# Feed-forward up and gate by Strassen's seven products, and the down projection as its own stage

## The chip, the core and the metric

The kernel runs on one core of a Trainium2 chip. The core has a matrix engine (PE, with its weight loads shown as PEld), a vector engine (DVE), a scalar engine for activations and copies (ACT), a general engine (POOL) and an engine that issues most transfers (SP). They work side by side, each in the order of its own instruction list, and wait for each other by semaphores. Data lies in SBUF (128 partitions), PE writes its sums to PSUM, and weights and results lie in DRAM.

The metric is the device time of one execution in microseconds (us), lower is better. Before the change it is 1745.42 us, the median of 3 runs (1744.86 to 1748.16).

## What is computed

One inference step of a one-layer encoder over 1024 prompt tokens and 8 streams of 16 tokens: T = 1152 tokens of width 1024. Attention, a short convolution and a cross-attention come first; the change touches what follows the last residual sum, the gated feed-forward with its causal convolution over time:

```python
D_MODEL = 1024; D_FF = 2816; FFN_CONV_WIDTH = 3

def rms_norm(x, g):
    y = x * lax.rsqrt(jnp.mean(x * x, axis=-1, keepdims=True) + EPS)
    return y * g

def causal_dwconv(u, state, w):             # three taps over time
    full = jnp.concatenate([state, u], axis=1)
    y = w[0] * full[:, 0:t_len]
    for j in range(1, 3):
        y = y + w[j] * full[:, j:j + t_len]
    return y, full[:, -2:]

    x = x + xo.reshape(b, t_len, D_MODEL) @ w_xo
    hf = rms_norm(x, g_ffn)
    u_c, new_ffn = causal_dwconv(hf @ w_up, ffn_state, w_ffconv)
    x = x + (jax.nn.silu(u_c) * (hf @ w_gate)) @ w_down
    ...
    y = rms_norm(x, g_final)
```

Everything is float32. The streams bring their own two earlier rows (`ffn_state`), the prompt starts from zeros, and the last two up-projected rows of each go out as `new_ffn`.

## The kernel before

Activations lie transposed, with 128 features on the partitions and the 1152 tokens along the free axis. A float32 product is made of three PE passes: each operand is split into a high part (rounded by ACT to PE's format, `h`) and a low part (`l = x - h`, on DVE or POOL), and `mm3` (L142 to L144) sums `h*h`, `h*l` and `l*h` in one PSUM bank. A weight unit is 128x1024 numbers (512 KB): one transfer `raw` into one of two buffers, then two halves, each a cast `wh` on ACT (L107) and a subtraction `wl` (L108), on POOL and DVE in turn. `block` multiplies one unit (eight 128x128 weight tiles for one block of 128 output features) with all tokens in three chunks of 384 columns (`CH`), 24 matmuls a chunk.

`residual` (L734) adds the output of the last projection (`w_xo`) to the residual `x`, writes the sum to DRAM (`x2`), and keeps it times the gain as split pairs `hfh`, `hfl`. The factor `r3` (one over the root mean square of a token) comes only after all of it is done, so it is multiplied in at the end of the up and gate products.

The feed-forward has 22 blocks of 128 hidden features. `ffn_block(f)` (L954) runs an up block, a convolution and a gate block:

- up: each bank is taken by DVE with `r3` into a padded row `u` (`evac_padded`, L249); the convolution is one ACT operation for the first tap (L261) and two DVE operations of 1168 columns (L263) for the others; ACT applies silu (L965), and POOL multiplies `r3` in (L967 for the prompt, L968 for the streams).
- gate: DVE multiplies each bank by this row (L978) and the product is split into the pair `gp`.

The blocks are gathered in groups (`GROUPS`, 4, 4, 4, 4, 3 and 3 blocks). Behind the first block of the next group stands the down projection of a finished one: `ffn_down` (L984) multiplies its pairs with the weights `w_dn` and adds to `acc` (8x1152 numbers a partition, kept in SBUF, L1000). `ffn_last` (L1011) makes the last group's share chunk by chunk (512, 384 and 256 columns) with the residual sums, their squares, and the final normalisation (`norm`, L1029), which is interleaved with the next chunk's products.

The program order is that of the Python code; the framework places each instruction in its engine's list by its own estimate of when it can run, adds the semaphore waits, and gives buffers out in turn from pools (for `raw` 2 buffers, for `wh` and `wl` 3 each). A transfer into a buffer waits until its last reader is done.

Of the kernel before, what the change touches and what calls it, by code (L numbers as in the profile page):

```python
# [33 lines left out]
GROUPS = [4, 4, 4, 4, 3, 3]  # L34
# [16 lines left out]
class Step:  # L51
    def __init__(self, ctx, tc, I, O):
# [5 lines left out]
        self.open("const")  # L58
        self.open("small")
# [5 lines left out]
    def open(self, name, side="left", space=None):  # L65
        kw = {} if space else {"side": side, "reuse_waits": "tile"}
# [28 lines left out]
    def bank(self, tag):  # L95
        return self.tile("psum", tag, [1024 if tag == "sc" else 512], 2)

    def const(self, shape, src, dt=F32):
        t = self.tile("const", f"c{self.n}", shape, 1, dt)
# [10 lines left out]
    def wraw(self, src, spare=None):  # L110
        raw = spare or self.tile("weights", "raw", [1024], 2)
# [3 lines left out]
    def wunit(self, src, spare=None):  # L115

        raw = self.wraw(src, spare)
        hs, ls = [], []
        for i in range(2):
            h, l = self.tile("weights", "wh", [512], 3, F32R), self.tile("weights", "wl", [512], 3, F32R)  # L120
            self.lflip ^= 1
            self.split(h, l, raw[:, i * 512:(i + 1) * 512], self.nc.gpsimd if self.lflip else self.nc.vector)
# [149 lines left out]
    def setup(self):  # L272
        nc, I = self.nc, self.I
        nc.scalar.preload_act_table_set("natural_log_exp_and_others")
        self.g = self.const([5, KT], I["gains"])
        self.ones = self.const([P], None)
        nc.vector.memset(self.ones, 1.0)
        self.eps = self.const([1], None)
# [6 lines left out]
    def setup2(self):  # L285
# [9 lines left out]
        self.wff = self.const([NFB, 3], I["wff"])  # L295
# [3 lines left out]
    def lam(self):  # L299

        nc = self.nc
        l = self.tile("const", "lam", [4], p=QD)
        nc.sync.dma_start(out=l, in_=self.I["lam"])
        pr = self.tile("const", "lampr", [2], p=QD)
# [13 lines left out]
    def start(self):  # L318
# [4 lines left out]
        self.r1 = self.tile("x", "r", [T])  # L323
# [410 lines left out]
    def residual(self, wsrc, xh, xl, xsrc, dst, gi, pool):  # L734
# [4 lines left out]
        r = self.tile(pool, "r", [T])  # L739
# [214 lines left out]
    def ffn_block(self, f):  # L954
        nc, I = self.nc, self.I
        u = self.A(TPAD)
        st, new = self.tile("t8", "sff", [NB, 2], 2), self.tile("t8", "nff", [18], 2)
        nc.sync.dma_start(out=st, in_=I["sff"][f])
        self.pads(u, st)
        self.block(I["w_ug"][2 * f], self.hfh, self.hfl, "mm", self.evac_padded(u, self.r3))  # L960
        self.last_rows(new, u)
        self.nc.sync.dma_start(out=self.O["nff"][f], in_=new)
        s = self.A(TPAD)
        self.conv(s, u, self.wff[:, f])
        nc.scalar.activation(s[:, HALO:TPAD], s[:, HALO:TPAD], AF.Silu)  # L965
        seg = self.pseg(s)[:, :, HALO:]
        nc.gpsimd.tensor_tensor(out=self.pp(s), in0=self.pp(s), in1=self.r3[:, 0:S_P], op=ALU.mult)  # L967
        nc.gpsimd.tensor_tensor(out=seg, in0=seg, in1=self.r3[:, S_P:T].rearrange("p (b t) -> p b t", t=TS), op=ALU.mult)  # L968
        gt = self.A()
        h, l = self.tile("t8", "gp", [T], 10, F32R), self.tile("t8", "gp", [T], 10, F32R)  # L970

        def evac(c, ps):
            cs = slice(c * CH, (c + 1) * CH)
            for bs, view, by_stream in self.chunk_views(s, c):
                a, o = ps[:, bs], gt[:, c * CH + bs.start:c * CH + bs.stop]
                if by_stream:
                    a, o = (z.rearrange("p (b t) -> p b t", t=TS) for z in (a, o))
                nc.vector.tensor_tensor(out=o, in0=a, in1=view, op=ALU.mult)  # L978
            self.split(h[:, cs], l[:, cs], gt[:, cs])

        self.block(I["w_ug"][2 * f + 1], self.hfh, self.hfl, lambda c: ("tr", "tr", "mm")[c], evac)
        return h, l

    def ffn_down(self, g, parts):  # L984
# [288 lines left out]
```

## Time and profile before

| | us |
|---|---|
| median of 3 runs | 1745.42 |
| the profiled execution's own time | 1758.31 |
| its span in the trace | 1756.3 |
| PE busy in the span | 1718.8 (98%) |
| DVE / ACT / POOL busy | 836.7 / 561.1 / 370.6 |
| mean granted clock of PE | 0.991 |

The profile comes from one execution, which took 12.9 us more than the median of the runs. In it the feed-forward starts at 892.8 us, when the last matmul of the residual stage is done. A busy engine is one that executes; waiting is not counted. A row of a group gives the line, the engine, the operation, the tiles out<-in with their shape, the count, the busy time and the mean duration of one; behind the second bar stands how long the engine was idle just before, and what ended that. PE overlaps its matmuls, so the duration of one (0.34 us at 384 columns) is not what the next has to wait; the time from one start to the next is.

### The profile page before, as it was taken

The numbers are of one execution on the slowest core, as the hardware profiler recorded it, in microseconds if no ns is written. First come the engines' busy times: TensorE is split into PE (matmuls) and PEld (weight loads), VectorE is DVE, ScalarE is ACT, GpSimd is POOL, SyncE is SP. The second block draws the span as 40 slices with busy tenths as digits, with TensorE's granted clock in tenths as the row PEclk, the third lists the DMA queues.
The fourth block names the chain that finished last, engine by engine and source line by source line (L and its number), as shares of the span: only waits on it lengthen the run. The fifth ranks groups of instructions, "written<-read, shape, count | busy, mean of one in ns | idle before, by whom it ended". The sixth has DMA issues, their size and how long they took to land.

```text
span 1756.3 us, 26026 instructions
## 1 busy us (share of the span) xinstructions
PE 1718.8 (98%) x10402; PEld 1657.5 (94%) x10402; DVE 836.7 (48%) x1486; ACT 561.1 (32%) x1149; POOL 370.6 (21%) x411
## 2 busy tenths in 40 slices
PE   8999989999999999999999999999999999999996
PEld 7999879999899999979999999999999999999995
DVE  8757546776733343473343333332333334234346
ACT  7222543654523332353342211220221122022144
POOL 3223332111123311102321111121211111121113
PEclk9999999999999999999999999999999999999998
DMA  5756876543274334623451111111111111111113
GB/s 195 257 197 211 284 238 192 162 112 111 82 283 141 122 120 177 236 79 113 135 161 56 38 49 37 49 49 37 38 49 37 40 47 49 37 38 49 37 37 108
DMA packets 84857, 196.92 MB, mean 112 GB/s; under 512 B 15488, under 2 KB 47104, under 8 KB 84736
## 3 DMA queue, kind: packets, MB, share of 16 engines
q1 hardware_dynamic: 83664, 193.62, 33.8%
q8 instruction: 82, 1.34, 0.3%
q10 hardware_dynamic: 1072, 1.64, 0.3%
q14 instruction: 39, 0.32, 0.1%
HBM read 150.81 MB, written 44.41 MB: 111 GB/s over the span
## 4 chain that ended last, share of the span: by engine, by line
PE 90%; DVE 5%; ACT 2%; DMA 1%; issue 1%; POOL 0%; SPq 0%; DVEq 0%; ACTq 0%; POOLq 0%
PE mm L142 15%; PE mm L144 15%; PE mm L143 15%; PE tr L142 7%; PE tr L143 7%; PE tr L144 7%; PE sc L142 5%; PE sc L143 5%; PE sc L144 5%; PE tr L644 2%; PE sc L605 1%; PE tr L631 1%; DVE acc L1029 1%; PE sc L512 0%; PE mm L806 0%
## 5 line engine op out<-in xcount | busy, mean ns | idle before, releaser
L108 POOL TENSOR_TENSOR wl<-raw,wh 128x512 fp32r<-128x512 f32 x118 | 154.3, 1308 | 1012.6 <-ACT wh L107 882.0
L107 ACT CAST wh<-raw 128x512 fp32r<-128x512 f32 x236 | 146.6, 623 | 597.3 <-PE mm L143 322.9
L142 PE MATMUL mm<-oh,wh 128*128 128x384 f32 x800 | 272.6, 341 | 0.0
L144 PE MATMUL mm<-oh,wl 128*128 128x384 f32 x800 | 270.7, 338 | 0.0
L143 PE MATMUL mm<-ol,wh 128*128 128x384 f32 x800 | 270.6, 338 | 0.0
L142 PE MATMUL mm<-xh,wh 128*128 128x384 f32 x496 | 169.8, 342 | 0.9 <-DVE t L813 0.9
L144 PE MATMUL mm<-xh,wl 128*128 128x384 f32 x496 | 167.9, 338 | 0.0
L143 PE MATMUL mm<-xl,wh 128*128 128x384 f32 x496 | 167.7, 338 | 0.0
L144 PE MATMUL sc<-gp,wl 128*128 128x384 f32 (+2 forms) x465 | 157.2, 338 | 0.0
L142 PE MATMUL sc<-gp,wh 128*128 128x384 f32 (+2 forms) x465 | 157.2, 338 | 0.0
L143 PE MATMUL sc<-gp,wh 128*128 128x384 f32 (+2 forms) x465 | 157.2, 338 | 0.0
L142 PEld LDWEIGHTS mm<-oh,wh 128*128 128x128 f32 x800 | 150.2, 188 | 1.8 <-issue 1.2
L142 PE MATMUL tr<-oh,wh 128*128 128x384 f32 x448 | 151.8, 339 | 0.0
L143 PE MATMUL tr<-ol,wh 128*128 128x384 f32 x448 | 151.5, 338 | 0.0
L144 PE MATMUL tr<-oh,wl 128*128 128x384 f32 x448 | 151.5, 338 | 0.0
L143 PEld LDWEIGHTS mm<-ol,wh 128*128 128x128 f32 x800 | 150.2, 188 | 0.5
L144 PEld LDWEIGHTS mm<-oh,wl 128*128 128x128 f32 x800 | 150.1, 188 | 0.0
L1000 DVE TENSOR_TENSOR acc<-sc,acc 128x384 f32<-128x384 f32 x120 | 66.9, 557 | 152.5 <-PE sc L144 152.5
L108 DVE TENSOR_TENSOR wl<-raw,wh 128x512 fp32r<-128x512 f32 x118 | 84.0, 712 | 111.7 <-ACT wh L107 111.7
L249 DVE TENSOR_TENSOR A<-mm,r 128x384 f32<-128x384 f32 (+1 forms) x88 | 38.3, 456 | 146.6 <-PE mm L144 146.5
L142 PEld LDWEIGHTS mm<-xh,wh 128*128 128x128 f32 x496 | 93.2, 188 | 3.7 <-issue 1.6
L143 PEld LDWEIGHTS mm<-xl,wh 128*128 128x128 f32 x496 | 93.3, 188 | 0.4
(342 smaller groups left out, 3459.0 us busy)
## 6 DMA issues: line engine op xcount, KB each, us to landing
raw<-in_w_ug SPq DMA_DIRECT2D x44, 512.0 KB, 3.5
raw<-in_w_dn SPq DMA_DIRECT2D x22, 512.0 KB, 3.5
kv<-in_kc SPq DMA_DIRECT2D x16, 512.0 KB, 5.4
kv<-in_vc SPq DMA_DIRECT2D x16, 512.0 KB, 5.9
qd<-qscr SPq DMA_DIRECT2D x64, 128.0 KB, 3.6
kv<-in_km SPq DMA_DIRECT2D x16, 512.0 KB, 5.7
kv<-in_vm SPq DMA_DIRECT2D x16, 512.0 KB, 5.5
raw<-in_w_bcx SPq DMA_DIRECT2D x12, 512.0 KB, 3.8
```

What stands on the lines that cost most here:

```text
L107: self.nc.scalar.copy(out=h, in_=x)
L108: (eng or self.nc.vector).tensor_tensor(out=l, in0=x, in1=fl(h), op=ALU.subtract)
L142: self.nc.tensor.matmul(out, lhsT=ah, rhs=bh, start=i == 0, stop=False)
L143: self.nc.tensor.matmul(out, lhsT=ah, rhs=bl, start=False, stop=False)
L144: self.nc.tensor.matmul(out, lhsT=al, rhs=bh, start=False, stop=i == n - 1)
L249: self.nc.vector.tensor_tensor(out=view, in0=a, in1=b, op=ALU.mult)
L605: nc.tensor.matmul(sc[:, a:b], lhsT=qd[:, m, hl, (i % 2) * P:(i % 2 + 1) * P], rhs=ks[m][:, a:b], start=hl == 0, stop=hl == 1)
L631: nc.tensor.transpose(tr[:, j * P:(j + 1) * P], a[:, kt * P:(kt + 1) * P], self.ident)
L644: nc.tensor.matmul(av[:, qs], lhsT=at[kt // 4][:, kt % 4, qs], rhs=vt[:, kt], start=kt == 0, stop=kt == n - 1)
L1000: nc.vector.tensor_tensor(out=a, in0=ps, in1=a, op=ALU.add)
L1029: eng.tensor_tensor(out=x, in0=x, in1=r, op=ALU.mult)
```

## The change

The weight units of two neighbouring blocks are taken together: they are a 2x2 matrix of quarters (two blocks of outputs by two halves of the 1024 inputs), and the tokens are cut in two halves of 576 (`HT`), so the activations are a 2x2 matrix as well. Instead of eight products of quarters, seven are formed (P1 to P7, in the form with fifteen sums), each with 4 weight tiles, 2 column chunks of 288 (`HC`) and 3 passes: 24 matmuls of 288 columns. The sums of weights (`S` tiles) are made on POOL for each pair; those of activations (`T1` to `T4`) once, behind the residual stage, on DVE, and split on ACT, DVE and POOL. Partial results meet in three PSUM double banks (`ch`): P1 in bank a, to which P2 is added after P1 has been copied out; P6 and P7 in bank b, with P4 (b, again); P5 and P3 in bank c. ACT copies and DVE adds (L1061) put them together in `u` or `g`.

The residual stage multiplies the sum not only by the gain but also by the factor `r` of an earlier normalisation; at its end DVE takes the reciprocal of `r` (L1005) and multiplies the new factor in (L1013), so that `r` corrects for both. POOL multiplies `u` (L1088) and the silu row (L1106) by `r`, over 1152 columns each. The convolution takes four DVE operations a row (L1104: 1024 and 128 columns, for two taps). The product of silu row and gate goes to DRAM (`gscr`, L1139) and the down projection runs after all of it, chunk by chunk over 512, 384 and 256 columns: it loads the pairs (`ffn_operand`, L1146) and all weights anew for each chunk, and adds 22 terms in one bank.

```diff
+    def residual_wino(self, wsrc, xh, xl, xsrc, dst, gi):
+        for n in range(KT):
+            j = n // 2 + 4 * (n % 2)
...
+                nc.vector.scalar_tensor_tensor(out=xg[j][:, cs], in0=x, scalar=self.g[:, gi, j:j + 1], in1=self.r[:, cs],
+                                               op0=ALU.mult, op1=ALU.mult)
+                self.sumsq(acc[:, cs], x, n == 0, sq=self.tile(self.tp, "sq", [CH], 2))
...
+                nc.vector.tensor_tensor(out=b11, in0=b12, in1=b11, op=ALU.subtract)
+                nc.vector.tensor_tensor(out=b12, in0=b22, in1=b12, op=ALU.subtract)
+                nc.vector.tensor_tensor(out=b22, in0=b22, in1=b11, op=ALU.subtract)
+                nc.vector.tensor_tensor(out=b21, in0=b21, in1=b22, op=ALU.subtract)
+                self.Tf[k] = {"T1": b11, "T2": b22, "T3": b12, "T4": b21}
+        nc.vector.reciprocal(out=self.r, in_=self.r)
...
+    def wino(self, raws, dst, first=False):
+        a11, a12 = raws[0][:, 0:512], raws[0][:, 512:1024]
+        a21, a22 = raws[1][:, 0:512], raws[1][:, 512:1024]
+        s3, s2, s4 = (self.tile("ws", "S", [512], 3) for _ in range(3))
+        tt = nc.gpsimd.tensor_tensor
+        tt(out=s3, in0=a11, in1=a21, op=ALU.subtract)
+        tt(out=a21, in0=a21, in1=a22, op=ALU.add)
+        tt(out=s2, in0=a21, in1=a11, op=ALU.subtract)
+        tt(out=s4, in0=a12, in1=s2, op=ALU.subtract)
+        opd = {"P1": (a11, "B11"), "P2": (a12, "B21"), "P3": (s4, "B22"), "P4": (a22, "T4"),
+               "P5": (a21, "T1"), "P6": (s2, "T2"), "P7": (s3, "T3")}
+        def product(p, c, start):
+            x, b = opd[p]
+            h, l = self.tile("weights", "wh", [512], 3, F32R), self.tile("weights", "wl", [512], 3, F32R)
+            self.split(h, l, x)
...
+                    for i, (w, y) in enumerate(((h, bh), (h, bl), (l, bh))):
+                        nc.tensor.matmul(o, lhsT=w[:, ks], rhs=y[:, ts], start=start and k == 0 and i == 0,
+                                         stop=k == 3 and i == 2, skip_group_check=True)
...
+        product("P1", "a", True)
+        nc.scalar.copy(out=sb(*p1), in_=bank("a"))
+        if first:
+            product("P2", "a", False)
+        product("P6", "b", True)
+        if not first:
+            product("P2", "a", False)
+        add(0, 1, "b", p1)
+        nc.scalar.copy(out=sb(0, 0), in_=bank("a"))
+        product("P7", "b", False)
+        product("P5", "c", True)
+        add(1, 1, "b", p1)
+        product("P4", "b", False)
+        add(1, 1, "c", (1, 1))
+        product("P3", "c", False)
+        add(1, 0, "b", p1)
+        add(0, 1, "c", (0, 1))
...
+    def ffn_conv(self, f, u):
...
+        nc.gpsimd.tensor_tensor(out=u[:, HALO:HALO + T], in0=u[:, HALO:HALO + T], in1=self.r, op=ALU.mult)
...
+        nc.scalar.activation(sp, u[:, 0:S_P], AF.Identity, scale=w[:, 0:1])
+        nc.scalar.activation(ss, v[:, :, 0:TS], AF.Identity, scale=w[:, 0:1])
+        for j in (1, 2):
+            for o, x in ((sp, u[:, j:j + S_P]), (ss, v[:, :, j:j + TS])):
+                nc.vector.scalar_tensor_tensor(out=o, in0=x, scalar=w[:, j:j + 1], in1=o, op0=ALU.mult, op1=ALU.add)
+        nc.scalar.activation(s, s, AF.Silu)
+        nc.gpsimd.tensor_tensor(out=s, in0=s, in1=self.r, op=ALU.mult)
...
+    def ffn_up(self):
+        for f in range(0, NFB, 2):
...
+            self.wino(cur, [halves(u, HALO) for u in us], f == 0)
+            ss = [self.ffn_conv(f + i, us[i]) for i in range(2)]
...
+            self.wino(cur, [halves(g) for g in gs])
+            for i in range(2):
+                nc.vector.tensor_tensor(out=gs[i], in0=gs[i], in1=ss[i], op=ALU.mult)
+                nc.sync.dma_start(out=self.gscr[:, f + i], in_=gs[i])
+
+    def ffn_operand(self, c, ks):
+        raw = self.tile(self.xp[1], "graw", [2, 512], self.xp[2])[:, :, 0:n]
+        self.nc.sync.dma_start(out=raw[:, 0:len(ks)], in_=self.gscr[:, ks[0]:ks[-1] + 1, a:b])
...
-    def ffn_block(self, f):
-    def ffn_down(self, g, parts):
-    def ffn_last(self, parts):
...
+        for c, (a, b) in enumerate(LAST):
...
+                for u in range(3):
+                    ws.append(self.wunit(I["w_dn"][j, :, u * 1024:min((u + 1) * 1024, DFF)]))
+                ps = self.bank("mm")[:, 0:n]
+                for k in range(NFB):
+                    if j == 0 and (c, k) not in self.gx:
+                        self.ffn_operand(c, [k, k + 1])
+                    h, l = (z[k % 8 // 4][:, k % 4 * P:(k % 4 + 1) * P] for z in ws[k // 8])
+                    terms.append((h, l, *self.gx[c, k]))
+                self.mm3(ps, terms)
```

What this does to the engines' lists is seen at three places. The first is DVE's list from the end of an up block to the gate block behind it, before the change (a steady block in the middle of the feed-forward; `A` are rows in SBUF, `mm` and `tr` PSUM banks):

```order
L249 TENSOR_TENSOR A_9341<-mm_9357,r_8210 128x384 [waits PE_49]
L249 TENSOR_TENSOR A_9341<-mm_9383,r_8210 128x384 [waits PE_49]
L108 TENSOR_TENSOR wl_9456<-raw_9449,wh_9455 128x512 [waits DMAHW5_49,PE_49,Activation_49]
L249 TENSOR_TENSOR A_9341<-mm_9409,r_8210 128x256 [waits PE_49]
L249 TENSOR_TENSOR A_9341<-mm_9409,r_8210 128x8x16
L263 SCALAR_TENSOR_TENSOR A_9439<-A_9341,c_99_486,A_9439 128x1168 [waits Activation_49]
L263 SCALAR_TENSOR_TENSOR A_9439<-A_9341,c_99_486,A_9439 128x1168 [waits DVE_49]
L978 TENSOR_TENSOR A_9446<-tr_9459,A_9439 128x384 [waits PE_49,Pool_49]
L108 TENSOR_TENSOR gp_9448<-A_9446,gp_9447 128x384 [waits Activation_49]
L978 TENSOR_TENSOR A_9446<-tr_9487,A_9439 128x384 [waits PE_49]
```

The same place after the change, in a steady pair (`ch` are the PSUM double banks, `s` the convolved row, `vs` the streams' part of `u`; the add into `g` takes P6 of the gate product out of bank b, and the `wl` behind it belongs to P7):

```order
L1061 TENSOR_TENSOR u_10231<-ch_10367,u_10231 128x576 [waits PE_49]
L112 TENSOR_TENSOR wl_10563<-raw_10235,wh_10562 128x512 [waits Activation_49]
L1104 SCALAR_TENSOR_TENSOR s_10462<-u_10231,c_8_83,s_10462 128x1024 [waits Activation_49]
L1104 SCALAR_TENSOR_TENSOR s_10462<-vs_10455,c_8_83,s_10462 128x128 [waits Activation_49]
L1104 SCALAR_TENSOR_TENSOR s_10462<-u_10231,c_8_83,s_10462 128x1024 [waits DVE_49]
L1104 SCALAR_TENSOR_TENSOR s_10462<-vs_10455,c_8_83,s_10462 128x128 [waits DVE_49]
L1104 SCALAR_TENSOR_TENSOR s_10481<-u_10232,c_8_83,s_10481 128x1024 [waits Activation_49]
L1104 SCALAR_TENSOR_TENSOR s_10481<-vs_10474,c_8_83,s_10481 128x128 [waits Activation_49]
L1104 SCALAR_TENSOR_TENSOR s_10481<-u_10232,c_8_83,s_10481 128x1024 [waits DVE_49]
L1104 SCALAR_TENSOR_TENSOR s_10481<-vs_10474,c_8_83,s_10481 128x128 [waits DVE_49]
L1061 TENSOR_TENSOR g_10490<-ch_10537,g_10491 128x576 [waits DMAHW7_49,PE_49,Activation_49]
L112 TENSOR_TENSOR wl_10593<-S_10496,wh_10592 128x512 [waits Activation_49]
```

Where two operations of the convolution stood ahead of the gate's first bank, eight now stand between the up product's last add and the add that clears bank b for P7 of the gate product.

ACT's list in the same pair: the cast is that of P2's weights, the four activations are the first tap of the two rows, and the copy into `g` takes P1 of the gate product out of bank a, to which P2 is added next.

```order
L111 CAST wh_10562<-raw_10235 128x512 [waits DVE_49,PE_49]
L1100 ACTIVATE s_10462<-u_10231,c_8_83 128x1024 [waits Pool_49]
L1101 ACTIVATE s_10462<-vs_10455,c_8_83 128x128 [waits Pool_49]
L1100 ACTIVATE s_10481<-u_10232,c_8_83 128x1024
L1101 ACTIVATE s_10481<-vs_10474,c_8_83 128x128
L1065 COPY g_10491<-ch_10507 128x576 [waits DMAHW5_49,PE_49]
L111 CAST wh_10592<-S_10496 128x512 [waits Activation_49]
```

The copy and the cast for P7's weights (`S_10496`) stand behind four activations, the first of which waits for POOL (the multiplication of `u` by `r`).

Behind the residual stage DVE's list goes on as follows after the change (the first 12 of 35 operations up to the add that frees bank b for the first P7; `xg` are sums of activations, `t` and `b` low parts of pairs, `c_9_84` is `r`):

```order
L985 TENSOR_TENSOR xc_9126<-tr_9101,xc_9126 128x384 [waits DMAHW3_49,DMAHW2_49,PE_49]
L112 TENSOR_TENSOR wl_9341<-S_9276,wh_9340 128x512 [waits Activation_49]
L987 SCALAR_TENSOR_TENSOR xg_9024<-xc_9126,c_6_79,c_9_84 128x384 [waits DVE_49]
L112 TENSOR_TENSOR t_9208<-xg_8316,t_9207 128x576 [waits Activation_49]
L1001 TENSOR_TENSOR xg_8910<-xg_9024,xg_8910 128x576 [waits DVE_49]
L112 TENSOR_TENSOR b_9139<-xg_9024,b_9138 128x576 [waits Activation_49]
L1005 RECIPROCAL c_9_84<-c_9_84 128x1152
L1002 TENSOR_TENSOR xg_9024<-xg_9024,xg_8910 128x576 [waits DVE_49]
L191 TENSOR_SCALAR xc_9150<-sc_9147 128x384 [waits DMAHW5_49]
L1003 TENSOR_TENSOR xg_9024<-xg_9024 128x576 [waits DVE_49]
L194 TENSOR_TENSOR xc_9150<-xc_9150,sq_9151 128x384 [waits DVE_49,Activation_49]
L112 TENSOR_TENSOR t_9212<-xg_8552,t_9211 128x576
```

Before the change this place held the three `r3` chunks and the splits of the last pairs. Now the rest of the list up to that add has ten more `t` operations of 576 columns, ten of 384 columns for the three chunks of `r`, and two `wl`; with those shown these are 16 operations of 576 columns, 14 of 384, three `wl`, the reciprocal of 1152 columns, and the add.

More of the change, by code (lines that the diff above doesn't have):

```diff
@@ L964, in ffn_block @@
[L964 to L979, printed above, removed]
@@ L981, in ffn_block @@
-        self.block(I["w_ug"][2 * f + 1], self.hfh, self.hfl, lambda c: ("tr", "tr", "mm")[c], evac)
-        return h, l
-    def ffn_down(self, g, parts):
-        nc, G = self.nc, GROUPS[g]
-        base = sum(GROUPS[:g])
-        units = {}
-        for j in range(KT):
-            if g == 0:
-                nc.sync.dma_start(out=self.acc[:, j], in_=self.x2[:, j])
-            for i in range(G * j, G * j + G):
-                if i // 8 not in units:
-                    units[i // 8] = self.wunit(self.I["w_dn"][base + i // 8])
-            for c in range(NCH):
-                cs = slice(c * CH, (c + 1) * CH)
-                ps = self.bank("sc")[:, 0:CH]
-                self.mm3(ps, self.down_terms(units, parts, j, cs))
-                a = self.acc[:, j, cs]
-                nc.vector.tensor_tensor(out=a, in0=ps, in1=a, op=ALU.add)
@@ new lines, in ffn_operand @@
+    def ffn_operand(self, c, ks):
+        a, b = LAST[c]
+        n = b - a
+        raw = self.tile(self.xp[1], "graw", [2, 512], self.xp[2])[:, :, 0:n]
+        self.nc.sync.dma_start(out=raw[:, 0:len(ks)], in_=self.gscr[:, ks[0]:ks[-1] + 1, a:b])
+        for i, k in enumerate(ks):
+            h, l = (self.tile(self.xp[0], "gx", [512], self.xp[3], F32R)[:, 0:n] for _ in range(2))
+            self.split(h, l, raw[:, i], (self.nc.vector, self.nc.gpsimd)[k % 4 == 3])
+            self.gx[c, k] = h, l
@@ L1033, in ffn_last @@
         wait = None
[L1034 removed]
+        for c, (a, b) in enumerate(LAST):
             n, end = b - a, b == T
[L1036 to L1037 removed]
+            ys = self.tile("t8", f"ys{c % 2}", [KT, 512 if c % 2 == 0 else CH])[:, :, 0:n]
+            sums = [self.tile("t8", "sum", [512], 4)[:, 0:n] for _ in range(2)]
             for j in range(KT):
[L1039 to L1041 removed]
+                x = ys[:, j]
+                nc.sync.dma_start(out=x, in_=self.x2[:, j, a:b])
+                ws = []
+                for u in range(3):
+                    ws.append(self.wunit(I["w_dn"][j, :, u * 1024:min((u + 1) * 1024, DFF)]))
+                ps = self.bank("mm")[:, 0:n]
+                terms = []
+                for k in range(NFB):
[4 more added lines that the diff above has]
+                self.mm3(ps, terms)
+                if j == (6 if end else 1) and wait:
```

214 lines of the change are left out of this document (138 added, 76 removed).

## The prediction

> **What bounds the kernel now.** I read the head of the page first, then its slices, then the chain that ended last: PE is busy 98% of the span, in the second half of the slices at 9 tenths throughout, and it holds 90% of the chain.
>
> ```profile
> span 1756.3 us, 26026 instructions
> PE 1718.8 (98%) x10402; PEld 1657.5 (94%) x10402; DVE 836.7 (48%) x1486; ACT 561.1 (32%) x1149; POOL 370.6 (21%) x411
> PE   8999989999999999999999999999999999999996
> PEclk9999999999999999999999999999999999999998
> PE 90%; DVE 5%; ACT 2%; DMA 1%; issue 1%; POOL 0%; SPq 0%; DVEq 0%; ACTq 0%; POOLq 0%
> ```
>
> Then the table by stages, for the feed-forward alone (us of the stretch, busy time and count of PE, PEld, DVE, ACT, POOL, clock, DMA), and the stall near its end (PE alone):
>
> ```profile
> 900.00:1700.00 800.00, 800.00 (x4525) 799.30 (x4524) 298.18 (x476) 169.69 (x244) 142.54 (x191) 1.00 0.15 47
> 893.00:900.00 7.00, 6.09 (x33) 5.42 (x32) 4.33 (x7) 3.78 (x8) 2.32 (x4) 1.00 0.84 255
> 1728.00:1731.60 3.60, 1.23 (x10) 1.00 1.02 376
> 1731.60:1735.10 3.50, 3.50 (x19) 0.51 0.57 210
> 1735.10:1738.50 3.40, 3.40 (x30) 1.00 0.01 2
> ```
>
> For 800 us PE never stops; the others are busy 37% at most and set nothing. 800.00 by 4525 is 176.8 ns from one matmul of 384 columns to the next. The feed-forward costs the number of its matmuls times their spacing, so fewer or narrower ones are saved in full, and whatever makes PE wait is paid in full. The row of 893 is the seam behind the residual stage, where PE lost 0.9 us. The last three rows show what a wait costs besides itself: the timeline of PE has
>
> ```profile
> 1727.05 0.28 PE L144 MATMUL sc<-gp,gp 128*128 128x256 f32 x1
> 1730.37 0.39 PE L142 MATMUL mm<-gp,gp 128*128 128x256 f32 x1 [3.04 <-DVE acc L1044]
> 1735.43 0.28 PE L144 MATMUL sc<-gp,gp 128*128 128x256 f32 x1
> 1735.55 0.28 PE L142 MATMUL sc<-gp,gp 128*128 128x256 f32 x1
> 1735.67 0.28 PE L143 MATMUL sc<-gp,gp 128*128 128x256 f32 x1
> ```
>
> so PE stood 3.3 us, and afterwards ran 3.5 us at a clock of 0.51, which is 1.7 us of work lost. Back at full clock, matmuls of 256 columns start 0.12 us apart (the last three rows).
>
> **Term 1, the seven products: -64 us (-76 to -54).** Before, 22 blocks times 2 times 72 are 3168 matmuls of 384 columns: 560 us at 176.8 ns. After, 22 calls times 7 times 24 are 3696 of 288. No row has that width. On the line between its neighbours, 120 ns at 256 and 176.8 at 384, lies 134 ns: 495 us. I take 131 and 137 as ends; the neighbours themselves would give 444 and 653, the second of which is a rival below.
>
> **Term 2, waits in each gate product: +55 us (23 to 66).** The order shows it: up's last add, a `wl`, then eight convolution operations on DVE, and only then the add that clears bank b for P7. Nothing in front of it waits for PE, so DVE runs it as fast as its inputs come. These rows price the chain:
>
> ```profile
> L263 DVE SCALAR_TENSOR_TENSOR A<-A,c,A 128x1168 f32<-128x1168 f32 x44 | 63.2, 1436 | 31.7 <-ACT A L261 31.0
> L978 DVE TENSOR_TENSOR A<-mm,A 128x128 f32<-128x128 f32 x22 | 6.2, 281 | 0.0
> L249 DVE TENSOR_TENSOR A<-mm,r 128x384 f32<-128x384 f32 x44 | 24.6, 558 | 126.9 <-PE mm L144 126.8
> L108 DVE TENSOR_TENSOR wl<-raw,wh 128x512 fp32r<-128x512 f32 x63 | 44.3, 703 | 49.5 <-ACT wh L107 49.5
> L967 POOL TENSOR_TENSOR A<-A,r 128x1024 f32<-128x1024 f32 x22 | 44.0, 2001 | 90.5 <-ACT A L965 90.5
> L968 POOL TENSOR_TENSOR A<-A,r 128x128 f32<-128x128 f32 x22 | 9.7, 442 | 0.0
> L261 ACT ACTIVATE A<-A,c 128x1168 f32<-128x1168 f32 x26 | 33.3, 1279 | 7.6 <-DVE A L249 5.2 <-POOL nff L268 2.4
> L965 ACT ACTIVATE A<-A 128x1168 f32<-128x1168 f32 x22 | 26.0, 1184 | 64.1 <-DVE A L263 64.1
> L107 ACT CAST wh<-raw 128x512 fp32r<-128x512 f32 x236 | 146.6, 623 | 597.3 <-PE mm L143 322.9
> ```
>
> Scaled by columns: a DVE add of 576 takes 0.76 us, a convolution operation 1.26 (1024) or 0.28 (128), POOL's multiplication of 1152 columns 2.2, ACT's first tap 1.13 and 0.25, an ACT copy of 576 some 0.7. Let up's last product end at 0. PE has P1, P6 and P2 of the gate (3.22 us each) and wants P2 at 6.4 and P7 at 9.65. DVE's add is done at 0.96, the `wl` at 1.65, POOL's `u` times `r` at about 3.95, ACT's four first taps from 4.0 to 6.8, its copy out of bank a at 7.55: P2 starts 1.2 us late. DVE's eight operations start at 5.2; if nothing disturbs them they take 6.2 us. But the first row is convolved at 8.3, silu done at 9.5, and POOL multiplies it by `r` from 9.8 to 12.1, while DVE stands at the second row. Rows where both engines read SBUF show what then happens, with two SBUF inputs on DVE, against one that comes from PSUM:
>
> ```profile
> L1029 DVE TENSOR_TENSOR acc<-acc,A 128x512 f32<-128x512 f32 x5 | 6.4, 1331 | 0.0
> L1029 POOL TENSOR_TENSOR acc<-acc,A 128x512 f32<-128x512 f32 x3 | 4.9, 1663 | 0.6 <-DVE A L189 0.6
> L1044 DVE TENSOR_TENSOR acc<-sc,acc 128x512 f32<-128x512 f32 x4 | 2.8, 690 | 2.1 <-PE sc L144 2.1
> ```
>
> 1331 ns against 690, and 1663 on POOL against the 1308 of its row below: they take turns. So the seventh operation waits for POOL until 12.1, the eighth ends at 13.6, the add at 14.4, P7's `wl` at 15.1. P7's third matmul, the first that needs it, starts at 15.1 where it could at 10: 5 us a pair, 55 for 11. Without taking turns the add ends near 12, which leaves 2.1 to 2.8 us; if POOL's weight sums (next row, four a call) fall in between as well, 6.
>
> ```profile
> L108 POOL TENSOR_TENSOR wl<-raw,wh 128x512 fp32r<-128x512 f32 x118 | 154.3, 1308 | 1012.6 <-ACT wh L107 882.0
> ```
>
> In this trace no long POOL operation fell on an L263 (its mean stays 1436), so the five us rest on L1029, which is the nearest row with two SBUF inputs; I take them. [...]
>
> **Term 3, the half clock behind those waits: +12 us (0 to 19).** A wait at P7 leaves PE idle for about 3.4 us in one piece, as the 3.3 us above did, and up to 1.7 us are lost after it, 11 times. One instance can't say that each wait of this length does it: I take two in three, 1.1 us a pair, and keep 0. [...]
>
> **Term 4, the start: +24 us (15 to 30).** Behind the last residual product DVE has 35 operations until bank b is free for the first P7, as the order shows: 16 of 576 columns (0.76), 14 of 384 (0.56), three `wl` (0.69) and the add are 22.8 us, and the reciprocal of 1152 columns comes on top.
>
> ```profile
> L618 DVE RECIPROCAL t<-t 128x1 f32<-128x1 f32 x32 | 5.1, 158 | 6.8 <-ACT p L617 6.3 <-ACT p L611 0.4
> L922 DVE RECIPROCAL t<-t 128x4 f32<-128x4 f32 x8 | 1.4, 177 | 6.6 <-ACT p L921 6.6
> ```
>
> Three columns more cost 19 ns, 6.3 a column: 7 us for 1152; at the speed of other operations (1 ns a column) 1.4. POOL's sums and splits may block up to 6. That makes 24 to 36 us, where PE has 9.65 us to do: 15 to 26 of waiting. I take 23, less the 0.9 lost at this seam before, and 2 for the half clock.
>
> **Term 5, up to down: +10 us (5 to 14).** The last products must be added, multiplied (1.4 us) and stored before SP comes to the loads behind that store in its list. A load of 512 KB takes 3.5 us:
>
> ```profile
> raw<-in_w_ug SPq DMA_DIRECT2D x44, 512.0 KB, 3.5
> raw<-in_w_dn SPq DMA_DIRECT2D x22, 512.0 KB, 3.5
> 1700.25 0.39 PE L142 MATMUL sc<-gp,gp 128*128 128x512 f32 x1
> 1700.47 0.39 PE L143 MATMUL sc<-gp,gp 128*128 128x512 f32 x1
> 1700.70 0.39 PE L144 MATMUL sc<-gp,gp 128*128 128x512 f32 x1
> ```
>
> The first pair is there 5 to 6 us late. The first output block then needs 22 casts of activations and 6 of weights on ACT, 28 times 0.623 or 17.4 us, where PE needs 66 matmuls of 512 columns, 0.23 us apart, or 15: 2 to 4 us more, and 1.7 for the half clock.
>
> **Term 6, the down products: +4 us (-1 to 12), and -5 at the end.** The same columns in the same passes: 528 matmuls each of 512, 384 and 256 are about what 1368 and the last group cost. In the 256-column chunk, 66 matmuls take 7.9 us, and three weight loads through two buffers (each held 3.5 us for the load, two casts and a split: 6.0) take 9.0: 8 times 1.1 at most, of which weights loaded ahead in the wider chunk hide some. The stall at 1727 (3.3 and 1.7) goes, since a block of 66 matmuls covers DVE's normalisation, where one of 9 did not. The stages before the feed-forward keep their order.
>
> **Sum.** -64 + 55 + 12 + 24 + 10 + 4 - 5 = +36 on the profiled 1758.3: 1794. The median is 0.7% below the profiled execution, so about 1781; I say **1780**.
>
> **Rivals.**
> - *Faster.* The convolution gets through undisturbed: waits of 2.1 us a pair and no half clock give 23 for 67, and the total falls to -8; with the start and the down stage at their low ends (-13), -21 to -25. From 1720 to 1740. It decides at 2.8 us a pair, where -64 + 24 + 10 + 4 - 5 is made up. For it: L263 was never slowed. Against: L1029.
> - *The change doesn't save.* If 288 columns take as long as 384 because the weight load (PEld, 94% busy) sets the spacing, 3696 times 176.8 are 653 us, +150 in place of -64: near 1990. Against: 256 columns run at 120.
> - *Weights late.* Each call needs two loads (3.5 us) and POOL sums (four of 1.3) after the call before has let go of the buffers; I find about 5 us of slack. If POOL taking turns with DVE eats it, 2 us in each of 22 calls: +44, near 1825.
>
> **Chances.** The forecast 0.62, the late weights 0.11, no saving 0.03, faster 0.18, and 0.06 in between. A measurement can tell 0.2% (3.5 us) from no change. Faster 0.18, same 0.06, slower 0.76. The range takes the lower half of the faster case as lost and ends inside the late weights: 1730 to 1820.
>
> **What would show it.** Right: a gap of 3 to 4 us before P7 in each gate product, released by the DVE add, with the L1104 operations ahead of it and some far over 1.26 us; a clock below 1 behind it; matmuls of 288 columns 134 ns apart. Wrong: PE near 100% busy between the start and the down stage, or gaps that end with a DMA or POOL.

## The result, and the profile after

The changed kernel takes 1812.07 us (median of 4 runs, 1811.21 to 1813.24) against 1745.14 us for the kernel before: a ratio of 1.0383, 95% interval 1.0365 to 1.0401. It is 67 us slower; 35 had been forecast (1780, range 1730 to 1820). The kernel before runs at 1743 to 1751 us in most executions and at 1757 to 1762 in others, its profiled ones among these; ratios of the later groups of runs move by half a per cent with the mixture.

The head of the page of the changed kernel, its slices, and the chain that ended last:

```profile
span 1810.2 us, 28157 instructions
PE 1687.9 (93%) x10930; PEld 1587.0 (88%) x10930; DVE 1027.9 (57%) x1553; ACT 678.2 (37%) x1385; POOL 613.3 (34%) x548
PE   8999989999999999999879999999999979999986
PEclk8999999999999999999989999999999989999999
PE 67%; DVE 8%; POOL 8%; DMA 7%; ACT 5%; issue 4%; SPq 0%; DVEq 0%; POOLq 0%; ACTq 0%
```

PE works 31 us less, and the execution is 54 us longer: PE's share fell from 98% to 93%, and of the chain it now holds two thirds instead of nine tenths. The chain's other parts are spread over DVE, POOL, DMA and ACT, so no single engine took PE's place. The table of stages of PE alone (us, busy and count, clock, DMA share, GB/s) shows where:

```profile
900.00:916.00 16.00, 1.95 (x4) 0.59 0.17 45
916.00:1479.40 563.40, 517.88 (x3696) 0.97 0.20 63
1479.40:1486.50 7.10, 0.21 (x2) 0.76 0.97 336
1486.50:1614.80 128.30, 125.42 (x528) 0.99 0.58 186
1614.80:1716.00 101.20, 95.81 (x532) 0.98 0.54 167
1716.00:1798.40 82.40, 68.96 (x531) 1.00 0.50 149
1798.40:1810.20 11.80, 1.94 (x10) 0.73 0.48 162
```

The same stages beside those of the kernel before. There up, gate and down products alternate, so up and gate are put at 560 us (3168 matmuls at 176.8 ns) and the rest of the 847.7 us of its feed-forward at down; its 0.9 us are what it lost at the third sum of squares, which stood a few matmuls behind the first up product:

| stage, us | before | after | difference |
|---|---|---|---|
| up to the end of the residual stage | 892.8 | 899.9 | +7.1 |
| wait at the start of the up products | 0.9 | 16.1 | +15.2 |
| up and gate products | 560.0 | 563.4 | +3.4 |
| from the last of them to the first down product | 0 | 7.1 | +7.1 |
| down products | 286.8 | 311.9 | +25.1 |
| after the last product | 15.8 | 11.8 | -4.0 |
| span | 1756.3 | 1810.2 | +53.9 |

Seven products in place of eight, and the stage that holds them is 3 us longer. The matmuls did get narrower at the expected rate, 0.13 us apart by the timeline of PE:

```profile
1169.71 0.29 PE L1051 MATMUL ch<-t,wh 128*128 128x288 f32 x1
1169.84 0.29 PE L1051 MATMUL ch<-t,wl 128*128 128x288 f32 x1
```

The median spacing over that stage is 133 ns, which makes 3696 times 133 or 492 us (the pure spacing); the other 72 us are waits and lost clock. The view of waits between 961 and 1479 (what PE waited for: total, times, longest):

```profile
PE ch L1051 <- DVE g L1061: 31.5, 10, 3.2
PE ch L1051 <- ACT g L1065: 6.7, 10, 0.7
```

Ten pairs, ten waits of 3.1 to 3.2 us on DVE's add into `g` and ten of 0.7 us on ACT's copy: P7 and P2 of the gate product. With the first pair (2.8 and 1.0 us) they are 34.3 and 7.6 us. No wait for weights, on a transfer or on POOL is among them. What DVE and POOL did before one of them, by their timelines:

```profile
1154.98 1.28 DVE L1104 SCALAR_TENSOR_TENSOR s<-u,c,s 128x1024 f32<-128x1024 f32 x1
1156.44 3.68 DVE L1104 SCALAR_TENSOR_TENSOR s<-u,c,s 128x1024 f32<-128x1024 f32 x1
1160.30 0.74 DVE L1061 TENSOR_TENSOR g<-ch,g 128x576 f32<-128x576 f32 x1
1156.35 2.68 POOL L1106 TENSOR_TENSOR s<-s,c 128x1152 f32<-128x1152 f32 x1
```

The same operation takes 1.28 us and, while POOL multiplies the silu row by `r`, 3.68. Nine of the eleven waits at P7 have a stretch at half clock behind them. In this pair, the wait, the 3.4 us ahead of the half clock, the half clock, and the 3.4 us after it:

```profile
1157.50:1161.10 3.60, 0.45 (x4) 1.00 0.00 0
1158.80:1162.20 3.40, 1.03 (x5) 1.00 0.02 2
1162.20:1165.60 3.40, 3.40 (x17) 0.50 0.00 0
1165.60:1169.00 3.40, 3.40 (x27) 1.00 0.54 154
```

There are 17 matmuls in the stretch at 0.50 and 27 in the next of the same length.

### The profile page after: what moved, and what is told of

Its sections match the earlier page's. It is cut to its first block, busy times and chain, and to the rows that moved or that the text cites. A ratio compares the mean times of both kernels' runs of the same rounds, so it can differ in the third digit from the quotient of the medians.

```text
span 1810.2 us, 28157 instructions
## 1 busy us (share of the span) xinstructions
PE 1687.9 (93%) x10930; PEld 1587.0 (88%) x10930; DVE 1027.9 (57%) x1553; ACT 678.2 (37%) x1385; POOL 613.3 (34%) x548
## 4 chain that ended last, share of the span: by engine, by line
PE 67%; DVE 8%; POOL 8%; DMA 7%; ACT 5%; issue 4%; SPq 0%; DVEq 0%; POOLq 0%; ACTq 0%
PE ch L1051 16%; PE mm L150 11%; PE mm L148 11%; PE mm L149 11%; PE tr L148 3%; POOL u L1088 3%; PE tr L149 3%; PE tr L150 3%; DMA raw<-in_w_ug 2%; DMA raw<-in_w_dn 2%; DMA graw<-gscr 2%; PE tr L653 2%; DVE wl L112 1%; PE sc L614 1%; ACT wh L111 1%
## 5 line engine op out<-in xcount | busy, mean ns | idle before, releaser
L1051 PE MATMUL ch<-t,wh 128*128 128x288 f32 x1408 | 297.0, 305 | 34.4 <-DVE g L1061 34.3
L112 DVE TENSOR_TENSOR wl<-raw,wh 128x512 fp32r<-128x512 f32 (+1 forms) x214 | 188.9, 883 | 224.8 <-ACT wh L111 220.9
L1051 PEld LDWEIGHTS ch<-t,wh 128*128 128x128 f32 x1408 | 236.8, 197 | 37.1 <-DVE g L1061 36.8
L1051 PE MATMUL ch<-b,wh 128*128 128x288 f32 x1056 | 215.3, 298 | 11.2 <-ACT g L1065 7.6
L1051 PE MATMUL ch<-t,wl 128*128 128x288 f32 x704 | 213.6, 306 | 2.2 <-DVE wl L112 1.7
L150 PE MATMUL mm<-gx,wl 128*128 128x512 f32 (+2 forms) x528 | 180.8, 342 | 16.2 <-POOL wl L112 9.7
L148 PE MATMUL mm<-gx,wh 128*128 128x512 f32 (+2 forms) x528 | 179.3, 340 | 10.7 <-ACT gx L111 8.0
L1051 PEld LDWEIGHTS ch<-b,wh 128*128 128x128 f32 x1056 | 170.4, 189 | 15.1 <-ACT g L1065 10.2
L149 PE MATMUL mm<-gx,wh 128*128 128x512 f32 (+2 forms) x528 | 179.6, 340 | 1.8 <-DVE gx L112 1.1
L1051 PE MATMUL ch<-b,wl 128*128 128x288 f32 x528 | 156.0, 295 | 0.0
L150 PEld LDWEIGHTS mm<-gx,wl 128*128 128x128 f32 x528 | 100.5, 190 | 27.3 <-POOL wl L112 13.3
L148 PEld LDWEIGHTS mm<-gx,wh 128*128 128x128 f32 x528 | 100.6, 191 | 21.9 <-ACT gx L111 10.1
L149 PEld LDWEIGHTS mm<-gx,wh 128*128 128x128 f32 x528 | 100.3, 190 | 13.1 <-DVE gx L112 3.8
L1104 DVE SCALAR_TENSOR_TENSOR s<-u,c,s 128x1024 f32<-128x1024 f32 x44 | 80.3, 1825 | 38.1 <-ACT s L1100 38.1
```

The costliest lines, as they stand in the source:

```text
L112: (eng or self.nc.vector).tensor_tensor(out=l, in0=x, in1=fl(h), op=ALU.subtract)
L148: self.nc.tensor.matmul(out, lhsT=ah, rhs=bh, start=i == 0, stop=False)
L149: self.nc.tensor.matmul(out, lhsT=ah, rhs=bl, start=False, stop=False)
L150: self.nc.tensor.matmul(out, lhsT=al, rhs=bh, start=False, stop=i == n - 1)
L1051: nc.tensor.matmul(o, lhsT=w[:, ks], rhs=y[:, ts], start=start and k == 0 and i == 0, stop=k == 3 and i == 2, skip_group_check=True)
L1104: nc.vector.scalar_tensor_tensor(out=o, in0=x, scalar=w[:, j:j + 1], in1=o, op0=ALU.mult, op1=ALU.add)
```

## The experiments

Each was measured beside the kernel before on the same chip; that kernel's median was 1749.45, 1759.37 and 1748.10 us in the three groups of runs below (the first four, the next four, the last two). Medians of different groups can differ by as much as that kernel's do, so the stages of the traces carry the comparisons.

**The kernel before, once more.**

> The kernel before, unchanged, to settle where its first profiled execution (1758.3 us) lost 13 us against its median of 1745. If transfers ahead of the feed-forward landed late in it, this execution comes at 1743 to 1750 us and its residual stage ends 8 to 13 us earlier than at 892.8 us, with the feed-forward (847.7 us) unchanged. If profiling itself costs that much, it comes near 1758 again. Either way the stages after 893 us should agree within 1 us.

1758.44 us again, and the two traces run within 2.3 us of each other from end to end, so which stage holds the 12 us was not seen. What can be told is how far the stages before the feed-forward move by themselves: with one list of instructions, the changed kernel's, the residual stage ended between 891 and 900 us in its trace and in those of the versions below that leave this stage alone. The +7.1 us of the table are inside that.

**The convolution emitted behind P7 of the gate product.**

> The convolution of a pair is emitted behind P7 of the gate product, so that the add that clears bank b stands ahead of the second row's four operations on DVE. My theory (the gate's waits are DVE's convolution ahead of that add, and the half clock follows from the 3.3 us gaps): the 11 waits of 3.1 us shrink below 0.7 us, the half-clock windows between 960 and 1480 us go, the total falls by 34 + 12 to 17 us, to 1758 to 1768 us. Rival (the copies on ACT or the weight sums on POOL are what P7 waits for): the waits keep their place with another releaser, and the total falls by less than 15 us. Second rival (half clock comes from something else): the waits go and the windows stay, 1775 to 1780 us.

```diff
         product("P7", "b", False)
+        if mid:
+            mid()
         product("P5", "c", True)
...
-            ss = [self.ffn_conv(f + i, us[i]) for i in range(2)]
+            ss = []
...
-            self.wino(cur, [halves(g) for g in gs])
+            self.wino(cur, [halves(g) for g in gs], mid=lambda: ss.extend(self.ffn_conv(f + i, us[i]) for i in range(2)))
```

1776.66 us, ratio 1.0134 (1.0084 to 1.0184), less gained than expected; up and gate take 529.6 us in place of 563.4. The waits on the add went; in their place PE waited on a low part, for P5. Its waits from 961 to 1437, and DVE's and POOL's timelines ahead of one (the added lines move the numbers: L1106 is DVE's convolution here, L1108 POOL's multiplication of the silu row):

```profile
PE ch L1051 <- DVE wl L112: 21.5, 11, 2.2
...
1089.92 2.77 DVE L1106 SCALAR_TENSOR_TENSOR s<-vs,c,s 128x128 f32<-128x128 f32 x1
1094.08 1.28 DVE L112 TENSOR_TENSOR wl<-raw,wh 128x512 fp32r<-128x512 f32 x2
1089.43 3.11 POOL L1108 TENSOR_TENSOR s<-s,c 128x1152 f32<-128x1152 f32 x1 [0.86 <-ACT s L1107]
```

An operation of 128 columns that takes 0.35 us alone took 2.77 beside POOL's 3.11, and the two `wl` behind it came late. The framework had placed the second row's operations ahead of them. Ten of these waits were 1.9 to 2.2 us long, and half-clock stretches followed 5 of the ten. So the mechanism was right and had only moved by one product.

**Without POOL's multiplication of the silu row.**

> Leaves out the multiplication of the silu row by r on POOL, so the hidden rows lack this factor. My theory (DVE's seventh convolution operation stands because POOL reads SBUF at the same time): L1104 with 1024 columns goes from a mean of 1825 ns to about 1280, the wait before P7 from 3.1 to about 0.8 us (26 us in 11 pairs), and with gaps that short the half clock goes too: 1765 to 1775 us; with the half clock left 1782 to 1788. Rival (the slow operation has another reason, as the order of operations on DVE alone): L1104 stays at 1825 and the total within 5 us of 1812.

The hidden rows lack this factor here, so the run is for its times alone. 1770.29 us, ratio 1.0105 (1.0073 to 1.0136). DVE's group, the waits between 916 and 1437, and the clock:

```profile
L1104 DVE SCALAR_TENSOR_TENSOR s<-u,c,s 128x1024 f32<-128x1024 f32 x44 | 56.4, 1281 | 38.6 <-ACT s L1100 38.6
...
PE ch L1051 <- ACT g L1065: 8.6, 11, 1.4
PE ch L1051 <- DVE g L1061: 8.0, 11, 0.8
...
961.00:1437.00 476.00, 460.57 (x3401) 1.00 0.22 71
```

1281 ns in place of 1825, waits of 0.7 us in place of 3.1, and a clock of 1.00 over that window: every number as the theory had it. The operations are in the same order on DVE, so order alone was not the cause; it is order together with POOL's multiplication beside them. What is left, 0.7 us each at P2 and P7, remains with this order when that multiplication is gone.

**Four raw buffers in the down stage.**

> The down stage gets four buffers for raw weights in place of two. Theory A (its 37 us over the pure spacing come from transfers that start only when a buffer is free): ACT's wait for raw weights (25 us between 1724 and 1784) goes, the 256-column chunk falls from 82 to about 66 us, the total by 15 to 20 us to 1792 to 1797. Theory B (the low parts are late, because a POOL and a DVE subtraction take turns): the total falls by less than 6 us, and PE goes on waiting for wl.

```diff
-                    ws.append(self.wunit(I["w_dn"][j, :, u * 1024:min((u + 1) * 1024, DFF)]))
+                    m = min(1024, DFF - u * 1024)
+                    spare = self.tile("t8", "raw2", [1024], 2)[:, 0:m] if (3 * j + u) % 2 else None
+                    ws.append(self.wunit(I["w_dn"][j, :, u * 1024:u * 1024 + m], spare))
```

**Low parts of the down weights on DVE alone.**

> In the down stage all low parts of weights are made on DVE, none on POOL; the two raw buffers stay. If the late weights come from POOL and DVE taking turns (a DVE wl there takes 1032 ns in place of 690, and the load waits for it), the 256-column chunk falls from 82 to 70 us or less, as with four raw buffers, and the total by 10 to 15. If the round of load, casts and splits over two buffers sets it whichever engine subtracts, the chunk stays above 78 us and the total within 6 us of 1812.

```diff
-            self.split(h, l, raw[:, i * 512:i * 512 + m], self.nc.gpsimd if self.lflip else self.nc.vector)
+            self.split(h, l, raw[:, i * 512:i * 512 + m], self.nc.gpsimd if self.lflip and not dve else self.nc.vector)
...
-                    ws.append(self.wunit(I["w_dn"][j, :, u * 1024:min((u + 1) * 1024, DFF)]))
+                    ws.append(self.wunit(I["w_dn"][j, :, u * 1024:min((u + 1) * 1024, DFF)], dve=True))
```

These two belong together: 1802.25 us (ratio 1.0276, 1.0226 to 1.0325) and 1796.95 us (1.0229, 1.0183 to 1.0275). In the changed kernel, ACT's waits and DVE's largest group in the 256-column chunk (1724 to 1784) were

```profile
ACT wh L111 <- DMA raw<-in_w_dn: 24.9, 14, 4.6
...
L112 DVE TENSOR_TENSOR wl<-raw,wh 128x512 fp32r<-128x512 f32 x13 | 13.4, 1032 | 16.8 <-ACT wh L111 13.1 <-PE mm L149 3.7
```

With four buffers ACT waits for PE instead, and the chunk takes 70.3 us; with DVE alone the low part takes 689 ns, ACT's wait for transfers stays, and the chunk takes 74.8 (the stage of each, then ACT's waits in it):

```profile
1717.20:1787.50 70.30, 65.64 (x533) 1.00 0.53 156
ACT wh L111 <- PE mm L149: 23.1, 28, 2.1
...
1706.30:1781.10 74.80, 68.16 (x531) 1.00 0.54 160
ACT wh L111 <- DMA raw<-in_w_dn: 25.1, 16, 2.7
```

Neither answer is the whole one, and both chunks lie between what the two theories expected. A weight buffer goes round through load, casts and subtractions. Without POOL in it the chunk falls from 82.4 us to 74.8, with four buffers to 70.3. Over the whole down stage both versions gain 11 us (311.9 to 301.2 and 300.7). The two effects are not separate ones: with four buffers DVE's `wl` was back at 692 ns, though POOL still made every other one. And whether POOL's part in the round is its own 1310 ns a `wl` or the 1032 that DVE then took was not told apart, since leaving POOL out removes both. With four buffers the seam between the gate and the down products lost 5 us of the gain: PE waited 12.0 us for the first operand, because both stores and a weight load into a new buffer stood ahead of its load in SP's list.

**The start.** The third sum of squares in a free bank:

> The third sum of squares behind the residual stage goes to a bank that is free, so PE does not wait for DVE (behind the reciprocal) before P1. My theory (DVE's list of 35 operations sets when P7 may start, whatever PE does before): P1 starts some 12 us earlier, but the add that frees bank b still comes 31 us after the residual stage, so the total changes by less than 3 us. Rival (the 12 us wait at the sums is the cost of the start): the total falls by 10 to 13 us.

```diff
-            ps = self.bank("sc")[:, :CH]
+            ps = self.bank(("sc", "sc", "mm")[c])[:, :CH]
```

And, on top of it, the reciprocal chunk by chunk in the last block of the residual stage, in place of one over 1152 columns:

> As the kernel with the free bank for the third sum, and the reciprocal of r is taken chunk by chunk in the last block of the residual stage, so that 4.9 of its 7.3 us stand beside PE's work. My theory (DVE's list is the bound): the add that frees bank b comes 5 us earlier than in the kernel with the sums alone, and the total falls by 4 to 8 us against it. Rival (the seam is bound by the copies on ACT or the sums on POOL): no difference above 2 us between the two.

```diff
+                if n == KT - 1:
+                    nc.vector.reciprocal(out=self.r[:, cs], in_=self.r[:, cs])
...
-        nc.vector.reciprocal(out=self.r, in_=self.r)
```

1808.01 us (ratio 1.0293, 1.0253 to 1.0333) and 1803.94 (1.0266, 1.0228 to 1.0303). DVE's reciprocal and the add that frees bank b, in the changed kernel, with the free bank, and with the early reciprocal (of the last, its third chunk):

```profile
L1005 DVE RECIPROCAL c<-c 128x1152 f32<-128x1152 f32 x1 | 7.3, 7341 | 0.0
930.91 0.75 DVE L1061 TENSOR_TENSOR u<-ch,u 128x576 f32<-128x576 f32 x1
...
927.44 0.74 DVE L1061 TENSOR_TENSOR u<-ch,u 128x576 f32<-128x576 f32 x1
...
895.74 2.54 DVE L990 RECIPROCAL c<-c 128x384 f32<-128x384 f32 x1
920.04 0.75 DVE L1062 TENSOR_TENSOR u<-ch,u 128x576 f32<-128x576 f32 x1
```

The residual stage's last matmul starts at 898.7, 894.8 and 891.5 us in these traces, so the add comes 32.2, 32.7 and 28.6 us after it. The bank alone does not bring the add forward (its 4 us in the median are against runs of another group); 4.8 us of reciprocal (7.34 less 2.54) taken off DVE's list bring the add 4.1 us earlier, P1 5.3 us earlier, and the median down by 4.1. DVE has no pause in its list from the last residual product to that add, so its list is the bound of the start. P1 itself did not come 12 us earlier with the free bank, as expected: it still waited (13.3 us, for ACT in place of DVE); the new PSUM banks are laid over those of the sums, which would explain it, but that was not tried.

**The convolution behind P5.**

> The convolution emitted one product later than in the first version of it (behind P5). In that version 11 waits of 2.2 us were left, at P5, whose wl stood behind the second row's four operations and POOL's multiplication in their midst; here P5's wl stands ahead of them and P4's behind. My theory: P5's waits go, at most 0.3 us is left at P4, no half clock between 960 and 1440 us, and the up and gate products from the first to the last take 512 to 520 us, where the changed kernel took 563 and the first version 533; the total is 15 to 25 us below the first version's. Rival (the waits follow the operations wherever they stand, since DVE is short of time in the gate product): as much wait at P4 as at P5 before, total within 5 us of the first version.

It is the first version's hook, one line lower. 1758.94 us, ratio 1.0011 (0.9989 to 1.0032): by the medians, which come from two groups, 18 us below the first version, by the stage 15.8. Waits between 961 and 1420, and the whole stage:

```profile
PE ch L1051 <- DVE g L1061: 10.0, 20, 0.6
907.60:1421.40 513.80, 499.52 (x3696) 1.00 0.22 69
```

Half a microsecond twice a pair is left (0.3 had been expected at most), the clock is 1.00, and up and gate take 514 us in place of 563: of the 72 us above the pure spacing, 50 are gone. DVE's operation of 128 columns beside POOL still takes 2.77 us here (at 1084.90); what stands behind it is now wanted later.

**All of it together**, and with four raw buffers from the second output block on:

> The three causes taken away together: the convolution behind P5, the free bank and the early reciprocal at the start, low parts of the down weights on DVE alone. If they are separate terms, their gains add: the version with the convolution behind P5 stood level with the kernel before on its chip (ratio 1.001), and minus 4 to 8 us at the start and minus 10 to 15 us in the down stage make a ratio of 0.987 to 0.992, faster than the kernel before. If they shared a cause (DVE's load), less than 8 us are gained beyond the convolution's place.

> As the version with the three causes taken away, with four raw buffers in the down stage from its second output block on. With both, the 256-column chunk should come to 64 to 68 us (63.4 is the pure spacing of 528 matmuls at 120 ns), 4 to 8 us below the version with two buffers, a ratio of 0.984 to 0.989. Rival (DVE's subtractions alone fed the chunk): no difference above 2 us between the two.

1745.85 us, ratio 0.9986 (0.9966 to 1.0005), and 1739.77 us, ratio 0.9948 (0.9929 to 0.9967). Both ratios miss the forecast ones (0.987 to 0.992 and 0.984 to 0.989): the first version is no more than level with the kernel before on this chip, the second half a per cent faster. The version with the convolution alone stood beside a kernel before at 1759.37, these two beside one at 1748.10, which would account for 0.6 per cent of the miss. The stages show that the gains do add: against the version with the convolution alone, the first of the two has P1 5.3 us sooner behind the residual stage and down products of 304.5 us in place of 315.5, both as expected; of these 16 us, 3.7 go again in longer up and gate products and a longer seam, and its residual stage ended 2.4 us later. The other's seam (the wait for the first operand) and its 256-column chunk:

```profile
1421.70:1431.00 9.30, 0.14 (x2) 0.62 0.85 307
...
1659.90:1728.60 68.70, 65.54 (x532) 1.00 0.55 161
```

The chunk takes 68.7 us, 7.6 less than in the version with two buffers (76.3), with 63.4 as the pure spacing.

## Why the prediction was right, and where its sizes were off

Direction, place and mechanism of the main loss came out as forecast. That the range held the time, near its upper end, is in part luck: that end stood there for late weights, which did not come. The down stage, the steps that had no price and the step to the median filled it instead, and waits and a start that were priced too high made up for part of them. By its own steps, in us of span:

| step | forecast | measured | how |
|---|---|---|---|
| 1, narrower matmuls | -64 | -68 | 133 ns spacing, 3696 of them |
| 2, waits in the gate product | +55 | +42 | 34.3 at P7, 7.6 at P2 |
| 3, half clock | +12 | +17 | the stage's half-clock stretches, 38 us at 0.24 us a matmul in place of 0.133 (3.8 of them at the start) |
| 4, the start | +24 | +18 | 15.2 to P1, 3.0 in waits behind it |
| 5, up to down | +10 | +15 | 7.1 to the first product, 8.4 in the first block |
| 6, down, and the end | -1 | +13 | 28.9 over the pure spacing in the last two chunks, -12.2 between that spacing and the 286.8 of before, tail -4.0 |
| not forecast | | +17 | 7 before the feed-forward, some 10 in small pauses |

- **Term 2** was right in its mechanism down to the operation: the seventh of the eight was held back by POOL, and leaving POOL's multiplication out released it. The waits on view are 3.8 us a pair in place of 5: the copy into `g` came 0.7 us late in place of 1.2, and the add 14.1 us behind up's last product in the pair shown, where I had 14.4. Part of the difference is only the count: from up's last product to P7's third matmul PE took 14.75 us in that pair, where 10.1 would do, so it was 4.6 us late; what the waits do not show of it is among the small pauses of the last row. That the two engines take turns, as the rows of L1029 had it, held for the convolution's operations too: 1.28 us alone, 3.68 beside POOL's 2.68.
- **Term 3** had 1.1 us a pair; a half-clock stretch of 3.4 us costs 1.5 and not the 1.7 of the forecast, since its matmuls start 0.24 us apart in place of 0.133, and nine of the eleven gate waits had one behind them or a longer one. The waits were 2.8 to 3.2 us long; the wait in the kernel before, too, reads 3.04 us of idle PE in its row, where the forecast speaks of 3.3. Waits of 1.9 to 2.2 us did it in 5 of ten cases (the first version of the experiments, at a clock of 0.98 from 961 to 1437), waits of 0.7 in none (the version without POOL's multiplication, at 1.00). Two in three was a guess. The traces of the kernel before and of the changed one say more: in each of them, from the start of the feed-forward on, all half-clock stretches begin a whole number of 3.413 us apart, as if on a grid (1111.0, 1162.2 and 1213.4 us in the changed kernel, for instance, are 15 steps apart). The waits of the changed kernel differ in how much of them falls into one step. In the pair shown above PE was busy 1.03 us of the step from 1158.8 to 1162.2, and the next ran at half clock. The wait that ended at 1010.0 was just as long, but the border of two steps cut it, and nothing followed:

```profile
1005.20:1008.60 3.40, 1.64 (x13) 1.00 0.03 5
1008.60:1012.00 3.40, 1.94 (x12) 1.00 0.02 2
```

  In the changed kernel the waits with a half clock behind them left PE idle for 1.87 us or more of one step, the two without one (the other ended at 1313.8) for 1.76 at most; in the kernel before, a step with 1.55 us of idle PE (226.4 to 229.8) had a half clock behind it all the same. That is read off the traces; no run moved a wait on purpose. For the forecast it is chance, then, that nine were hit: the pairs came some 51 us apart, nearly 15 steps, so most of the waits fell alike.
- **Term 4**: the list of 35 operations was the bound, as the two experiments at the start show, and the reciprocal took 7.3 us, where 7 was the higher of two prices. The sequence on PE was not foreseen: PE stood 11.8 us at the third sum, with P1 behind it, and hardly at P7.
- **Term 6 is the one that failed.** I priced the 256-column chunk by a round of 6.0 us a buffer, 9.0 us an output block, took half of what that is over 7.9 for hidden, and gave nothing for the 384-column chunk. The chunks took 128.3, 101.2 and 82.4 us, where 528 matmuls at the measured 227, 173 and 120 ns make 119.9, 91.3 and 63.4. The eight blocks of the last chunk, by their first matmuls, took 13.1, 9.1, 8.8, 9.5, 9.0, 10.5, 11.5 and 10.8 us. The middle four (9.1 on average) are the round as priced, and none of it is hidden: 5 us. The other 14 of the 19 us over the pure spacing lie in the first block and the last three, which had no term. In the first, ACT once waits 4.6 us for a load; in the last, DVE spends 5.85 us (from 1791.63) on the normalisation of the chunk before, and PE waits 2.6 us for the low part behind it; what held the other two was not followed. The slow subtractions that I had used for term 2 and left out here (a `wl` of 1032 ns on DVE in place of 690) are part of this: without POOL in the round the chunk took 74.8 us. The 384-column chunk lost 9 of its 10 us in its first three blocks (14.3, 13.0 and 16.0 us, where 11.4 would do), to operands that were still being split and to the normalisation of the chunk before, as DVE's and POOL's timelines have it:

```profile
1646.83 7.43 DVE L1167 TENSOR_TENSOR ys<-ys,nt 128x512 f32<-128x512 f32 x5
1646.88 5.16 POOL L1167 TENSOR_TENSOR ys<-ys,nt 128x512 f32<-128x512 f32 x3 [3.68 <-DVE nt L195]
1652.00 3.40 POOL L112 TENSOR_TENSOR wl<-raw,wh 128x512 fp32r<-128x512 f32 x2
```

  Both engines turned to it at once, and PE waited 2.7 us for the `wl` that stands behind it on POOL.
- **From the profiled time to the median** I took 0.7% off, because the kernel before ran that much faster without the profile. The changed kernel's profiled execution (1811.96 us) lies at its median, so 14 of the 32 us between forecast and result come from this step. Where the kernel before loses or saves these 13 us stays open.

Of the rivals, the faster one had its condition (the convolution gets through) right: the experiment behind P5 meets it, with waits of 0.5 us, and saves 50 us in the stage. But with the start and the down stage as they were that was level with the kernel before, not faster: the decisive point was at 2.8 us of wait a pair only with a down stage that costs little. Matmuls as slow as before are ruled out by the 133 ns, and late weights by the waits between 961 and 1479 us, none of which is for weights.

## What to carry to other kernels

Where one engine is busy 98% of the time, work taken off it is only won if the chains it now waits for fit in the shorter time: price the helper engines' lists between two of its instructions, as they are ordered, and count DVE operations with two inputs in SBUF and POOL's as taking turns, as they did here (the convolution's took 3.68 us in place of 1.28, a `wl` 1.03 in place of 0.69). A short wait can cost half as much again in clock behind it (1.5 us behind one of 3.1), so where an instruction stands in a helper's list can be worth nearly as much as arithmetic: the convolution emitted five products later brought 50 us, the narrower matmuls 68. A stage that loads its weights anew must be priced as a round of a buffer, with none of it hidden (9.1 us a block in the middle of the last chunk, where 9.0 had been priced and the matmuls alone take 7.9), and its first and last blocks need terms of their own (14 of that chunk's 19 us).

## What the runs showed of the hardware

Half-clock stretches of 3.4 us, in which matmuls of 288 columns started 0.24 us apart in place of 0.133, stood behind waits of PE of 1.9 to 3.2 us: nine of the eleven waits of 2.8 to 3.2 us had one, and five of the ten of 1.9 to 2.2 us in the first version. From the start of the feed-forward on, the stretches of both kernels begin a whole number of 3.413 us apart; in the changed kernel half clock followed each step of that length that PE idled for 1.87 us or more, and no stretch began behind one of 1.77 or less, while in the kernel before one began behind 1.55. DVE's reciprocal took 6.4 to 6.6 ns a column (7.34 us for 1152, 2.54 for 384), 4.5 times an addition of 384 columns (0.56 us). And a very short DVE operation was no safer beside POOL than a long one: one of 0.35 us took 2.77, while POOL's operation beside it took 3.11.
